# Hybrid trunk layer on one core: tile 8's left half last, a ring of three left blocks, evenly paced weight sums

## The chip, the cores and the metric

The kernel runs on one core of one Trainium2 chip. Times are device microseconds of one launch, the median of several runs. TensorE (PE) multiplies matrices, VectorE (DVE) and ScalarE (ACT) work on SBUF and PSUM, GpSimd (POOL) on SBUF; DMAs are issued from the queues of SyncE (SP), ACT and POOL. The engines run beside one another and wait by semaphores; each works through its own instructions in order.

## What is computed

One layer of a diffusion trunk on 9 tiles of 128 tokens: tiles 0 to 7 are the 1024 latent tokens, tile 8 holds 128 context tokens. The layer normalises and modulates its input, projects it, forms a gated chunk MLP (group A) and a 4-head latent attention (group B), and ends with one output projection. Only the attention and this end matter here:

```python
p = jax.nn.softmax(s, axis=-1)                       # s: 1024 latent + 256 cached keys
attn = jnp.einsum('bhqk,bkhv->bqhv', p, v_all)
y = jnp.concatenate([a_out, attn * silu(g_b)], axis=-1) @ w_o     # 1024 x 1024
out = x + gate * y                                    # gate by condition: latent or context
y_final = rmsnorm(out, final_g)                       # over the 1024 columns
```

## The kernel before

Every product in float32 is made of three matmuls: each operand is split into a high part (a cast, fp32r) and a low part (the rest), and high x high, high x low and low x high are summed in PSUM. `lo_of` (L112, DVE) makes a low part; the high part is a cast on ACT or `pool_copy` (L115) on POOL.

**Output projection.** The mixed activations lie in `mixA` (group A) and `mixB` (group B), transposed. Tiles 0 to 7 form four pairs. A pair's 2 x 2 block product with `w_o` (token tile x half of the inputs, against half of the inputs x half of the columns) is done by Strassen and Winograd's scheme with 7 products in place of 8. A product has 4 steps of 128 inputs, each 3 matmuls of 128x512 (`three`, L1909 to L1911), 12 in all. Its left block is a block of activations (`A11`, `A12`, `A22`) or a sum of blocks (`S1` to `S4`, made on POOL by `s_sums`); its right block is a quarter of `w_o` (`B11`, `B21`, `B22`) or one of four combinations `T1` to `T4`. Results are added up as `c11`, `c12`, `c21`, `c22`, then gated (`m..`), added to `x` (`a..`), squared with a row sum (`sq`), normalised (`norm`) and scaled by `final_g` (`y`, L2110). Tile 8 has no partner: `out_terms` (L1938 to L1940) does it with 8 steps of 3 matmuls for each half of 512 columns, early, as filler between the last attention heads.

**Left blocks.** `ring(q)` gives product q one of five SBUF slots for its high and low part; the cast into it, a copy `raw` into PSUM (L2136) and the subtraction (L112) come ahead of the product.

**Weight combinations.** `t_unit` makes T1 to T4 during attention in 8 units (u) of two half steps. A unit has four subtractions on POOL (L809), two casts on ACT into `thi` (L1883), two low parts on DVE in place in `traw`, and eight stores to `tdram` on SP (L1880). `divide` runs once per head and calls one or two half steps in turn. After the units, the rows of `w_o` are loaded (`wo_piece`, L1653) through one raw buffer at a time and split, two pieces per head (`spare_hi`, `spare_lo`). The combinations come back by DMAs on POOL's queue: `t_fetch` (L1901) for T3 and `t_piece` (L1905) for the others.

**Order.** In attention, one list of steps for PE sets the order, with due times (`later`) for what other engines do. After attention a small planner (`Plan.run`) goes through the steps with their costs, dependencies and priorities and writes each engine's instructions in that order; nothing is reordered when it runs. Pieces of tile 8 and of the first two products (`early`, one piece is 3 matmuls) stand among the last heads' matmuls.

**The end.** The last product, `A22` of pair 3, is done in two pieces of 256 columns, and tile 7's sum of squares is completed with the second.

Of the kernel before, what the change touches and what calls it, by code (L numbers as in the profile page):

```python
# [94 lines left out]
def tile_hymba_step(ctx: ExitStack, tc: tile.TileContext, I, O):  # L95
# [1371 lines left out]
    units, traw, unit_of, paced = [], {}, [], [0]  # L1467
    s2 = pss.tile([P, 2, 256], F32, tag="s2", name="s2", bufs=1)

    def softmax(t, h, lat_, con_):  # L1470
# [22 lines left out]
        def divide():  # L1493
            V.tensor_tensor(rs, su[:, 0:1], su[:, 1:2], op=ALU.add)
            V.reciprocal(rs, rs)  # L1495
            G.tensor_scalar(e, e, rs, 0.0, op0=ALU.mult, op1=ALU.add)  # L1496
# [140 lines left out]
    raw_free = [True]  # L1637
# [6 lines left out]
    def next_load():  # L1644
        if not loads or (loads[0][0] < 5 and not raw_free[0]):
            return
        k, hi, lo = loads.pop(0)
        if k < 5:
            raw_free[0] = False
            r = wo.tile([P, 1024], F32, tag="wor", name=f"wor{k}", bufs=1)  # L1650
        else:
            r = ap_.tile([P, 1280], F32, tag="e", name=f"wor{k}", bufs=6)[:, :1024]
        nc.sync.dma_start(r, I["w_o"][k])  # L1653

        def low(c_):
            lo_of(lo[:, c_], r[:, c_], hi[:, c_])
            if c_.start and k < 5:
                raw_free[0] = True
                next_load()
# [123 lines left out]
    with tc.manual_schedule(engines=engines):  # L1783
# [11 lines left out]
        EARLY = (("A11", "B11"), ("A12", "B21"), ("S4", "B22"), ("S2", "T2"), ("S1", "T1"), ("S3", "T3"), ("A22", "T4"))  # L1795
        FINAL = (("A11", "B11"), ("A12", "B21"), ("S2", "T2"), ("S1", "T1"), ("S3", "T3"), ("S4", "B22"), ("A22", "T4"))
        queue = [(n, *blk) for n in range(4) for blk in (FINAL if n == 3 else EARLY)]
# [19 lines left out]
        def ring(q):  # L1817

            i = q % 5
            if i not in slots:  # L1820
# [3 lines left out]
                    3: lambda: flat[0][4], 4: lambda: wo.tile([P, 1024], F32R, tag="ml", name="ringA", bufs=2),  # L1824
# [22 lines left out]
        def need_lo(key):  # L1847
            while key not in made:
                if los:
                    spare_lo(1)  # L1850
                else:
# [3 lines left out]
                    now[0] = now_  # L1855

        th, tl = {}, {}
# [7 lines left out]
        def t_unit(u, part):  # L1865
# [3 lines left out]
            b11, b12, b21, b22 = (raw[:, i, :] for i in range(4))  # L1869
            if part == 0:  # L1870
# [5 lines left out]
            hi = tp.tile([P, 4, 256], F32R, tag="hi", name=f"thi{u}")  # L1876

            def store(i, src):
                for m, j in ((1, 0), (3, 1), (4, 2), (2, 3)):
                    nc.sync.dma_start(f32(tdram[m - 1, k][:, i, 256 * c : 256 * c + 256]), src[:, j, :])  # L1880

            def high(i):
                S.copy(hi[:, 2 * i : 2 * i + 2, :], raw[:, 2 * i : 2 * i + 2, :])  # L1883
                if i:
                    store(0, f32(hi))

            def low(i):
                lo_of(raw[:, 2 * i : 2 * i + 2, :].bitcast(F32R), raw[:, 2 * i : 2 * i + 2, :], hi[:, 2 * i : 2 * i + 2, :])
                if i:
                    store(1, raw)  # L1890
                    if u + 2 < 8:
                        t_load(u + 2)

            for i in range(2):
                later(3.2 + 1.8 * i, lambda i=i: high(i))
                later(4.6 + 1.8 * i, lambda i=i: low(i))
# [48 lines left out]
        for c in range(len(pairs)):  # L1945
# [18 lines left out]
            if 2 * c + LEAD + 1 == 17:  # L1964
                assert not units
                closed(c_tp)
                c_wo, wo = opened("wo", side="left")
                for k in range(2):
                    wo_piece(k, *flat[0][2 * k : 2 * k + 2])
# [12 lines left out]
        wps[8] = [psw.tile([P, 512], F32, tag="w", name=f"w8{i}") for i in range(2)]  # L1982
        first_banks = [psw.tile([P, 512], F32, tag="w", name=f"f{i}") for i in range(2)]

        def load_xr(t):
            xr[t] = ep.tile([P, 1024], F32, tag="xr", name=f"xr{t}", bufs=4)
            nc.sync.dma_start(xr[t], I["x"][t])

        def plain(k, i):
            out_terms(8, wps[8][i], 512 * i, 512 * i + 512, [k])  # L1990
            if k == 4 and i == 1:
                for n in range(4):
                    t_fetch(3, n, woh[n][:, 512:1024], wol[n][:, 512:1024])

        early = []
        for k in range(7):
            early += [(0.65, lambda i=i, k=k: plain(k, i)) for i in range(2)]
            if k < 4:
                early.append((0.65, lambda k=k: product(0, first_banks[0], ks=[k])))
            elif k < 6:  # L2000
                early.append((0.65, lambda k=k: product(1, first_banks[1], ks=[k - 4])))
# [33 lines left out]
    def on_g(key, fn, deps, prio, cost=1.3, **kw):  # L2035
        step(key, "G", cost, fn, deps, prio, lag=0.15, **kw)
# [8 lines left out]
    def load_gate(cond, **kw):  # L2045
        gate[cond] = ep.tile([P, 1024], F32, name=f"gate{cond}", **kw)
        nc.sync.dma_start(
            gate[cond].rearrange("p (j r) -> p j r", j=4), gdram.rearrange("j (c r) -> c j r", c=2)[cond : cond + 1].broadcast_to([P, 4, 256])
        )

    for m, n in ((1, 0), (4, 4)):
        for k in range(4):
            fetch(f"T{m}{k}", lambda m=m, k=k, n=n: t_piece(m, k, tpiece[n + k]))
        if m == 1:
            fetch("gate0", lambda: load_gate(0, tag="gate0"))
    fetch("gate1", lambda: load_gate(1, tag="xr", bufs=4))
    for t in (8, 0, 1):
        fetch(f"x{t}", lambda t=t: load_xr(t))
    fetch("fg", lambda: nc.sync.dma_start(fg, I["final_g"].broadcast_to([P, 1024])))
# [9 lines left out]
    groups = {t: g for g in ((8,), (0, 1), (2, 3), (4, 5), (6,), (7,)) for t in g}  # L2069

    def square(t, j, junk, c, deps, prio=3.0, src=None):
        g = groups[t]

        def go():
            if g not in ssq:
                ssq[g] = sm.tile([P, 4], F32, tag="fss", name=f"fss{t}", bufs=3)
# [12 lines left out]
    def norm(g, prio, by_half=False):  # L2089
# [16 lines left out]

        for i, u in enumerate(g):
# [5 lines left out]
            if not by_half:  # L2113
                on_v(f"y{u}", scale, [*prev, "fg"], prio, 1.25)

        def scale_half(c):
            S.activation(xr[t][:, c], xr[t][:, c], AF.Copy, scale=ssq[g][:, 0:1])  # L2117
            nc.scalar.dma_start(O["y"][t][:, c], xr[t][:, c])

        if by_half:  # L2120
            for h_, c in (("L", L), ("R", R)):
                on_s(f"y{t}{h_}", lambda c=c: scale_half(c), [*prev, f"fg{t}{h_}"], 1.5)
# [4 lines left out]
    for q in range(3, len(queue)):  # L2127
# [4 lines left out]
        room = {3: ["pl7"], 4: ["pl7"], 5: []}.get(q) if q < 6 else [name_of(q - 5)]  # L2132
# [20 lines left out]
    def finish_plain():  # L2153
        for j, c in enumerate((L, R)):
            ps = wps[8][j]
            on_v(f"g8{j}", lambda ps=ps, c=c: V.tensor_tensor(ps, ps, gate[1][:, c], op=ALU.mult), ["pl7", "gate1"], 3.0)
            on_v(f"a8{j}", lambda ps=ps, c=c: V.tensor_tensor(xr[8][:, c], ps, xr[8][:, c], op=ALU.add), [f"g8{j}", "x8"], 3.0)
            square(8, j, lambda ps=ps: ps, c, [f"a8{j}"])
        step("free8", "N", 0.0, lambda: None, ["sq8.0", "sq8.1"], 0, gives=("w", "w"))
        norm((8,), 3.5)  # L2160
# [3 lines left out]
    def pair(n):  # L2164
# [3 lines left out]
        last = n == 3  # L2168
# [3 lines left out]
        q0 = 7 * n  # L2172
        at_ = {queue[q0 + i][1]: q0 + i for i in range(7)}
# [7 lines left out]
        for i in range(6 if last else 7):  # L2181
            q = q0 + i
            name = queue[q][1]
            m = queue[q][2]
            deps = [f"lo{q}", *([f"{m}{k}" for k in range(4)] if m[0] == "T" else [])]
            if n == 0 and i < 2:
                banks[name] = first_banks[i]
                if i == 0:
                    plan.made[P_(name)] = plan.made["|" + P_(name)] = 0.0
                    continue  # L2190

                def rest(q=q, name=name):
                    product(q, banks[name], ks=[2])
                    for h_ in range(2):
                        plain(7, h_)
                    plan.made["pl7"] = 2.4
                    product(q, banks[name], ks=[3])

                on_t(P_(name), 2.75, rest, [])
                continue  # L2200

            def whole(q=q, name=name):
                bank(name)
                product(q, banks[name])

            on_t(P_(name), 2.73, whole, deps, takes=("w",))

# [3 lines left out]
        if last:  # L2211
            on_v(D_("m11"), lambda: V.tensor_tensor(banks["A12"], banks["A12"], gate[0][:, L], op=ALU.mult), [D_("c11")], 2)
            on_v(D_("a11"), lambda: V.tensor_tensor(xr[a][:, L], banks["A12"], xr[a][:, L], op=ALU.add), [D_("m11"), f"x{a}"], 2)
            square(a, 0, lambda: banks["A12"], L, [D_("a11")])
            step(f"free{n}", "N", 0.0, lambda: None, [f"sq{a}.0"], 0, gives=("w",))
        else:
# [195 lines left out]
```

## Time and profile before

| | |
|---|---|
| median of 3 runs | 629.32 us (628.65 to 631.04) |
| the profiled execution | 629.55 us, its span 627.8 us |
| PE busy | 600.1 us (96%) |
| DVE, ACT, POOL busy | 68%, 53%, 35% |
| mean granted PE clock | 0.992 |
| attention, heads | until about 536 us |
| output products | PE's last matmul ends at 615.78 us |

Times in the profile count from the span's start. "Busy" is the time in which an engine executes; the idle time before an instruction is given with what released it, in square brackets in the timeline. An engine that is idle costs time only if PE, or the last chain, waits for it.

### The profile page before, as it was taken

To read this page: it belongs to the slowest core of one execution; us is meant where nothing else is said; L and a number is where in the kernel's file an instruction comes from. 1 tells how busy PE (TensorE), PEld (TensorE's weight loads), DVE (VectorE), ACT (ScalarE), POOL (GpSimd) and SP (SyncE) were. 2 spreads that over 40 slices of the span, in tenths; PEclk is the share of its full clock that TensorE was granted. 3 is DMA by queue.
4 is the path that set the end of the run, shared out by engine and by line. 5 is a ranking of instruction groups with operands and counts; after the bars stand their busy time and mean duration, and the time that the engine had idled before them with its cause. 6 is when DMAs were issued, how large, how long until landed. Compare 5 with 4: busy or idle time off the path is not lost. (4 is left out here: it accounts for less than half of the span.)

```text
span 627.8 us, 10196 instructions
## 1 busy us (share of the span) xinstructions
PE 600.1 (96%) x3659; PEld 538.9 (86%) x3659; DVE 427.5 (68%) x911; ACT 329.9 (53%) x765; POOL 218.1 (35%) x261
## 2 busy tenths in 40 slices
PE   8899999999999999999999989899999999989992
PEld 7578889999989999999988978789999988768882
DVE  4784458896855567566778677786766855458765
ACT  6556754336423354555675656566555443456543
POOL 2451111000000000433462455552332566558772
PEclk9999999999999999999999999999999999989997
DMA  8992000101261034000020063651101028944222
GB/s 318 389 367 72 1 33 2 34 1 67 101 232 62 11 119 131 13 1 1 6 69 1 27 215 130 202 167 35 68 2 34 33 85 267 367 154 168 88 101 114
DMA packets 31922, 67.33 MB, mean 107 GB/s; under 512 B 3440, under 2 KB 18560, under 8 KB 31360
## 3 DMA queue, kind: packets, MB, share of 16 engines
q1 hardware_dynamic: 28560, 57.50, 26.5%
q0 software_dynamic: 2880, 8.39, 4.1%
q10 hardware_dynamic: 432, 0.79, 0.3%
q8 instruction: 29, 0.48, 0.3%
q14 instruction: 21, 0.17, 0.1%
HBM read 53.45 MB, written 13.21 MB: 106 GB/s over the span
## 5 line engine op out<-in xcount | busy, mean ns | idle before, releaser
L1496 POOL TENSOR_SCALAR e<-e,rs 128x1280 f32<-128x1280 f32 x32 | 46.2, 1444 | 105.5 <-DVE rs L1495 49.3
L112 DVE TENSOR_TENSOR pl<-pT,ph 128x512 fp32r<-128x512 f32 x81 | 55.4, 687 | 39.3 <-ACT ph L1561 37.9
L1490 ACT ACTIVATE e<-s,nb,scl 128x256 f32<-128x256 f32 x64 | 56.1, 880 | 39.8 <-DVE nb L1484 39.8
L1561 ACT CAST ph<-pT 128x512 fp32r<-128x512 f32 x80 | 46.0, 587 | 35.4 <-PE pT L1557 31.7
L1237 POOL TENSOR_TENSOR kr<-z,rope 128x64 f32<-128x64 f32 x8 | 2.6, 322 | 172.5 <-ACT z L1246 172.5
L1557 PE MATMUL pT<-ident,e 128*128 128x128 f32 x320 | 48.4, 274 | 6.8 <-DVE pl L112 6.8
L752 PE MATMUL tp<-area,w 128*128 128x384 f32 x288 | 52.4, 338 | 0.0
L752 PEld LDWEIGHTS tp<-area,w 128*128 128x128 f32 x288 | 50.3, 188 | 0.4
L1581 PE MATMUL o<-ph,vh 128*128 128x256 f32 x160 | 47.7, 298 | 0.0
L1557 PEld LDWEIGHTS pT<-ident,e 128*128 128x128 f32 x320 | 37.1, 140 | 12.1 <-PE at L1600 4.0
L1583 PE MATMUL o<-ph,vl 128*128 128x256 f32 x160 | 45.2, 282 | 0.0
L1582 PE MATMUL o<-pl,vh 128*128 128x256 f32 x160 | 45.1, 282 | 0.0
L1480 DVE TENSOR_REDUCE m<-s 128x1 f32<-128x1024 f32 x32 | 38.9, 1216 | 1.5 <-PE s L1514 1.5
L1510 PE MATMUL s<-kch,area 128*128 128x512 f32 (+2 forms) x100 | 39.0, 390 | 0.0
L1513 PE MATMUL s<-krh,area 128*128 128x512 f32 (+2 forms) x100 | 35.4, 354 | 0.0
L1511 PE MATMUL s<-kcl,area 128*128 128x512 f32 (+2 forms) x100 | 35.3, 353 | 0.0
L1512 PE MATMUL s<-kch,area 128*128 128x512 f32 (+2 forms) x100 | 35.2, 352 | 0.0
L1514 PE MATMUL s<-krl,area 128*128 128x512 f32 (+2 forms) x100 | 35.2, 352 | 0.0
L976 PE MATMUL tp<-area,w 128*128 128x384 f32 x192 | 35.0, 337 | 0.0
L976 PEld LDWEIGHTS tp<-area,w 128*128 128x128 f32 x192 | 33.6, 188 | 0.4 <-issue 0.4
L1581 PEld LDWEIGHTS o<-ph,vh 128*128 128x128 f32 x160 | 30.4, 190 | 1.6
L1582 PEld LDWEIGHTS o<-pl,vh 128*128 128x128 f32 x160 | 30.4, 190 | 1.4
(660 smaller groups left out, 1731.3 us busy)
## 6 DMA issues: line engine op xcount, KB each, us to landing
ada<-in_ada_ss SPq DMA_DIRECT2D x16, 512.0 KB, 8.5
w2r<-in_w_t SPq DMA_DIRECT2D x12, 512.0 KB, 4.5
x<-in_x SPq DMA_DIRECT2D x9, 512.0 KB, 7.9
xr<-in_x SPq DMA_DIRECT2D x9, 512.0 KB, 8.5
adag<-in_ada_g SPq DMA_DIRECT2D x4, 1024.0 KB, 5.0
traw<-in_w_o SPq DMA_DIRECT2D x16, 256.0 KB, 3.4
tdram<-thi SPq DMA_DIRECT2D x32, 128.0 KB, 3.0
tdram<-traw SPq DMA_DIRECT2D x32, 128.0 KB, 2.1
```

Of the source, the lines that this page charges most:

```text
L112: V.tensor_tensor(lo, src, f32(hi), op=ALU.subtract)
L752: T.matmul(tps[i, g][:, :GW], w_[i][:, k, :], x_[k, g], start=k == 0 and j == 0, stop=k == NK - 1 and j == 2)
L976: T.matmul(tps[c, 2][:, :GW], w_[c][:, k, :], x_[k, 2], start=k == 0 and m == 0, stop=k == NK - 1 and m == 2)
L1480: V.tensor_reduce(m[:, 0:1], lat_, axis=AX.X, op=ALU.max)
L1490: S.activation(e[:, sl], src, AF.Exp, bias=nb, scale=scl[:, t : t + 1], accum_out=su[:, i : i + 1])
L1496: G.tensor_scalar(e, e, rs, 0.0, op0=ALU.mult, op1=ALU.add)
L1510: T.matmul(ps, qh_, kch[:, sl], start=True, stop=False)
L1557: T.transpose(ps[:, w : w + P], es[t, h][:, c * P : (c + 1) * P], ident)
L1561: later(0.5, lambda: S.copy(ph[:, :w], ps[:, :w]))
L1581: T.matmul(o, vh[:, kt, :], ph[:, sl], start=c == 0, stop=False)
L1582: T.matmul(o, vh[:, kt, :], pl[:, sl], start=False, stop=False)
L1583: T.matmul(o, vl[:, kt, :], ph[:, sl], start=False, stop=c == n - 1)
```

## The change

It does these things:

- `t_unit`: `divide` calls one half step per head, always. `thi` becomes two tiles of half the size; each half is stored by two DMAs as soon as it is made. The raw rows of `w_o` open after the last unit, wherever that falls, and are read through two buffers instead of one (`raw_free` holds two tags).
- Tile 8's right half stays among the early pieces; its left half is moved behind the last product, in two pieces of 256 columns. Three steps of the third product join the early pieces. The early list has 17 pieces instead of 20.
- `ring` has three slots instead of five (the slot of tile 8's own high part stays taken until the end). A product's left block waits for the product three before it.
- The order of the products is written out for the first nine (`FIRST`): pair 1's first two products come ahead of pair 0's `A22`.
- C21 stays in its PSUM bank and is gated and added to `x` there by DVE, for all pairs, instead of POOL in SBUF.
- `gate0`, tile 8's gate and input (`own1`), `x0`, `x1` and `final_g` are loaded from ACT's queue instead of SP's, later in the order; tile 8's gate and input are loaded by halves.
- Tiles 6 and 7 are normalised together, and the last sums are those of tile 8.

What it does to the order at three places. SP's stores and loads in the weight sums, before (`tdram<-thi` are the high parts, `tdram<-traw` the low parts, `traw<-in_w_o` the next unit's rows):

```order
L1880 DMA tdram<-thi_4268 128x256 x4
L1880 DMA tdram<-traw_4113 128x256 x4
L1863 DMA traw_4368<-in_w_o 128x2x256 x2
L1880 DMA tdram<-thi_4354 128x256 x4
L1880 DMA tdram<-traw_4275 128x256 x4
L1863 DMA traw_4452<-in_w_o 128x2x256 x2
```

and after:

```order
L1876 DMA tdram<-thi_4354 128x256 x2
L1876 DMA tdram<-traw_4095 128x256 x2
L1876 DMA tdram<-thi_4385 128x256 x2
L1876 DMA tdram<-traw_4095 128x256 x2
L1867 DMA traw_4416<-in_w_o 128x2x256 x2
```

A unit's stores are the same eight, in pairs, and two tiles of high parts take turns.

POOL at the end of attention, before (`area` and `kch`, `krh` are places of `w_o` rows, `tp`, `vht`, `vlt` those of T1 and T4):

```order
L1905 DMA area_120<-tdram 128x1024 x4
L115 TENSOR_SCALAR kch_5755<-wor_5757 128x512 x2
L115 TENSOR_SCALAR krh_5759<-wor_5761 128x512 x2
L115 TENSOR_SCALAR area_120<-wor_5763 128x512
L1901 DMA area_118<-tdram 128x512 x4
L1901 DMA area_119<-tdram 128x512 x4
L115 TENSOR_SCALAR area_120<-wor_5763 128x512
L115 TENSOR_SCALAR ringC<-mixB 128x512
L1905 DMA tp_6044<-tdram 128x1024
L1905 DMA tp_6045<-tdram 128x1024
L1905 DMA tp_6046<-tdram 128x1024
L1905 DMA tp_6047<-tdram 128x1024
```

```order
L806 TENSOR_TENSOR mixA<-mixA,mixB 128x4x128
L1905 DMA tp_6048<-tdram 128x1024
L809 TENSOR_TENSOR mixB<-mixA 128x4x128
L1905 DMA tp_6049<-tdram 128x1024
L809 TENSOR_TENSOR mixA<-mixA 128x4x128
L1905 DMA vht<-tdram 128x1024
L809 TENSOR_TENSOR mixB<-mixB 128x4x128
L1905 DMA vlt<-tdram 128x1024
```

and after, from the same place:

```order
L115 TENSOR_SCALAR area_120<-wor_5771 128x512 x2
L1911 DMA area_118<-tdram 128x512 x4
L1911 DMA area_119<-tdram 128x512 x4
L115 TENSOR_SCALAR ringC<-mixB 128x512
L1915 DMA tp_6043<-tdram 128x1024
L1915 DMA tp_6044<-tdram 128x1024
L1915 DMA tp_6045<-tdram 128x1024
L1915 DMA tp_6046<-tdram 128x1024
L1915 DMA tp_6047<-tdram 128x1024
L1915 DMA tp_6048<-tdram 128x1024
L1915 DMA vht<-tdram 128x1024
L1915 DMA vlt<-tdram 128x1024
```

The fetches of T1 and T4 stand in one run, and pair 1's sums come behind them.

DVE at the end, before (L2283, L2284 gate and add the last product's two pieces; L2254, L2255 are tile 6's, L2300 is tile 7's output):

```order
L2110 SCALAR_TENSOR_TENSOR xr_6349<-xr_6349,fss_6485,fg 128x1024
L2110 SCALAR_TENSOR_TENSOR xr_6371<-xr_6371,fss_6485,fg 128x1024
L2263 TENSOR_TENSOR P_3_6665<-S_3_6630,gate_6100 128x512
L2267 TENSOR_TENSOR S_3_6630<-S_3_6630,gate_6100 128x512
L2268 TENSOR_TENSOR xr_6532<-S_3_6630,xr_6532 128x512
L2266 TENSOR_TENSOR xr_6532<-P_3_6665,xr_6532 128x512
L806 TENSOR_TENSOR S_3_6652<-S_3_6652,mixB 128x512
L2283 TENSOR_TENSOR A_3_6670<-A_3_6670,gate_6100 128x256
L2254 TENSOR_TENSOR S_3_6652<-S_3_6652,gate_6100 128x512
L2284 TENSOR_TENSOR A_3_6670<-A_3_6670,xr_6532 128x256
L2283 TENSOR_TENSOR A_3_6670<-A_3_6670,gate_6100 128x256
L2255 TENSOR_TENSOR xr_6510<-S_3_6652,xr_6510 128x512
```

and after (`left` is tile 8's left half, `own_6610` its gate and input, `A_3` the last product):

```order
L806 TENSOR_TENSOR A_3_6633<-A_3_6633,mixA 128x512
L2221 TENSOR_TENSOR A_3_6633<-A_3_6633,gate_6094 128x512
L2222 TENSOR_TENSOR xr_6514<-A_3_6633,xr_6514 128x512
L2273 TENSOR_TENSOR left<-left,own_6610 128x256
L2098 TENSOR_TENSOR smalls<-smalls,fss_6586 128x2
L2274 TENSOR_TENSOR left<-left,own_6610 128x256
```

```order
L2120 SCALAR_TENSOR_TENSOR xr_6491<-xr_6491,fss_6586,fg 128x1024
L2273 TENSOR_TENSOR left<-left,own_6610 128x256
L2277 TENSOR_SCALAR smalls<-smalls 128x1
L2274 TENSOR_TENSOR left<-left,own_6610 128x256
L2281 SCALAR_TENSOR_TENSOR smalls<-fss_6187,smalls 128x1
L2283 RECIPROCAL rlast<-smalls 128x1
```

Tile 6's output scaling (L2120) now stands ahead of the last piece's gating; tile 7's work is ahead of it.

The diff, cut to its core:

```diff
-                n_ = min(len(units), (1, 2)[paced[0] % 2])
+                n_ = 1
                 paced[0] += 1
-                for _ in range(n_):
-                    unit_of[0](*units.pop(0))
+                for i in range(n_):
+                    unit_of[0](*units.pop(0), 2.2 * i)
...
-    raw_free = [True]
+    raw_free = ["wor", "ml"]
...
+        FIRST = ((0, "A11"), (0, "A12"), (0, "S4"), (0, "S2"), (0, "S3"), (0, "S1"), (1, "A11"), (1, "A12"), (0, "A22"))
+        LATER = {1: ("S1", "S2", "S4", "S3", "A22"), 2: ("A11", "A12", "S2", "S1", "S4", "S3", "A22"), 3: ("A11", "A12", "S2", "S1", "S3", "S4", "A22")}
...
-            i = q % 5
+            i = q % 3
             if i not in slots:
                 slots[i] = {
                     0: lambda: flat[0][5], 1: lambda: wo.tile([P, 1024], F32R, tag="ml", name="ringB", bufs=2),
                     2: lambda: wo.tile([P, 1024], F32R, tag="wor", name="ringC", bufs=1),
-                    3: lambda: flat[0][4], 4: lambda: wo.tile([P, 1024], F32R, tag="ml", name="ringA", bufs=2),
...
+            def store(i, part_, src):
+                for m, j in ((1, 0), (3, 1), (4, 2), (2, 3))[2 * i : 2 * i + 2]:
+                    nc.sync.dma_start(f32(tdram[m - 1, k][:, part_, 256 * c : 256 * c + 256]), src[:, j % 2, :])
+
+            def high(i):
+                his_[u, i] = tp.tile([P, 2, 256], F32R, tag=f"hi{i}", name=f"thi{u}{i}")
+                S.copy(his_[u, i], raw[:, 2 * i : 2 * i + 2, :])
+                store(i, 0, f32(his_[u, i]))
...
+            for dt, fn, i in ((3.2, high, 0), (4.6, low, 0), (5.0, high, 1), (6.4, low, 1)):
+                later(dt + more, lambda fn=fn, i=i: fn(i))
...
+        early = [(0.65, lambda k=k: plain(k)) for k in range(4)]
+        early += [(0.65, lambda k=k: product(0, first_banks[0], ks=[k])) for k in range(4)]
+        for k in range(3):
+            early.append((0.65, lambda k=k: plain(4 + k)))
+            early.append((0.65, lambda k=k: product(1, first_banks[1], ks=[k])))
+        early += [(0.65, lambda k=k: product(2, first_banks[2], ks=[k])) for k in range(3)]
...
+    def load_gate():
+        gate[0] = ep.tile([P, 1024], F32, name="gate0", tag="gate0")
+        nc.scalar.dma_start(
...
-            on_v(D_("c21"), lambda: add(V, K, ps("A22"), K), [P_("A22"), D_("k7")], 2, gives=("w",))
-            on_g(D_("m21"), lambda: G.tensor_tensor(K, K, gL(), op=ALU.mult), [D_("c21"), "gate0"], 3)
-            on_g(D_("a21"), lambda: add(G, half(b, L), half(b, L), K), [D_("m21"), f"x{b}"], 3)
...
+            on_v(D_("c21"), lambda: add(V, ps("A22"), ps("A22"), K), [P_("A22"), D_("k7")], 2)
+            on_v(D_("m21"), lambda: V.tensor_tensor(banks["A22"], banks["A22"], gate[0][:, L], op=ALU.mult), [D_("c21"), "gate0"], 2.5)
+            on_v(D_("a21"), lambda: V.tensor_tensor(xr[b][:, L], banks["A22"], xr[b][:, L], op=ALU.add), [D_("m21"), f"x{b}"], 2.5)
...
+        def left(j, c):
...
+            out_terms(8, cell["o"][:, c], c.start, c.stop, range(8))
+
+        for j, c in enumerate((slice(0, 256), slice(256, 512))):
+            on_t(f"pz{j}", 2.9, lambda j=j, c=c: left(j, c), [], takes=("w", "w") if j == 0 else ())
+            on_v(f"zm{j}", lambda c=c: V.tensor_tensor(cell["o"][:, c], cell["o"][:, c], g()[:, c], op=ALU.mult), [f"pz{j}", "own0"], 0.5, 0.42)
+            on_v(f"za{j}", lambda c=c: V.tensor_tensor(cell["o"][:, c], cell["o"][:, c], x()[:, c], op=ALU.add), [f"zm{j}"], 0.5, 0.42)
```

More of the change, by code (lines that the diff above doesn't have):

```diff
@@ L1644, in next_load @@
     def next_load():
-        if not loads or (loads[0][0] < 5 and not raw_free[0]):
+        if not loads or (loads[0][0] < 5 and not raw_free):
             return
@@ L1657, in low @@
             if c_.start and k < 5:
[L1658 removed]
+                raw_free.append(tag)
                 next_load()
@@ L1875, in t_unit, with open_wo @@
             sub(G, b21, b21, b22)
[L1876 to L1896, printed above, removed]
+            for dt, fn, i in ((3.2, high, 0), (4.6, low, 0), (5.0, high, 1), (6.4, low, 1)):
+                later(dt + more, lambda fn=fn, i=i: fn(i))
+        def open_wo():
+            nonlocal c_wo, wo
+            closed(c_tp)
+            c_wo, wo = opened("wo", side="left")
+            for k in range(2):
+                wo_piece(k, *flat[0][2 * k : 2 * k + 2])
         def t_fetch(m, k, hi, lo):
@@ L2179, in bank @@
             banks[name] = psw.tile([P, 512], F32, tag="w", name=f"{name}_{n}")
[L2181 to L2206, printed above, removed]
+        bank_of[n] = bank, banks
         s_done = [f"s{m}{n}" for m in range(4)]
```

278 lines of the change are left out of this document (141 added, 137 removed).

## The prediction

> **What bounds the kernel now.** I read the page first, then the waits of PE, then busy time by stretch, then the timeline at each gap and the chain that ended last. The page says that PE is the engine that matters, and that no other is near full:
>
> ```profile
> PE 600.1 (96%) x3659; PEld 538.9 (86%) x3659; DVE 427.5 (68%) x911; ACT 329.9 (53%) x765; POOL 218.1 (35%) x261
> ```
>
> So time is won or lost only where PE stands still, and after its last matmul. The stretches show where (columns: PE, PEld, DVE, ACT, POOL busy, PE clock, DMA share, GB/s):
>
> ```profile
> 350.00:360.00 10.00, 10.00 (x70) 9.12 (x70) 6.16 (x14) 6.61 (x14) 4.21 (x5) 1.00 0.08 28
> 360.00:380.00 20.00, 17.39 (x118) 15.55 (x117) 15.36 (x30) 12.03 (x26) 10.66 (x11) 1.00 0.62 198
> 380.00:400.00 20.00, 19.50 (x136) 17.74 (x135) 14.71 (x26) 11.94 (x26) 11.96 (x13) 1.00 0.48 159
> 400.00:430.00 30.00, 27.50 (x189) 24.93 (x189) 22.77 (x45) 17.97 (x38) 13.41 (x13) 1.00 0.51 158
> 430.00:500.00 70.00, 70.00 (x491) 64.63 (x489) 50.27 (x105) 39.24 (x83) 23.58 (x24) 1.00 0.09 31
> 540.00:560.00 20.00, 17.33 (x68) 13.21 (x67) 12.52 (x20) 9.14 (x20) 13.35 (x13) 0.91 0.77 272
> 560.00:616.00 56.00, 55.78 (x258) 46.49 (x256) 41.41 (x75) 30.32 (x72) 39.57 (x28) 1.00 0.35 122
> 616.00:627.80 11.80, 0.00 (x0) 0.00 (x0) 5.39 (x20) 4.41 (x13) 2.53 (x2) 0.71 0.24 89
> ```
>
> Three losses lie in what the change touches. PE idles 2.61 + 0.50 + 2.50 = 5.6 us between 360 and 430, where the weight sums run, and nothing in the 70 us after. It loses 2.7 us at 540 to 560. It ends at 615.78 (0.22 short of 616), and 12.0 us follow without it. The profiled execution took 629.55 us, 0.23 above the median of the runs, with 1.75 us around its span of 627.8; the sum below is made against 629.55.
>
> **1. Weight sums in attention: one half step per head, stores by halves.** What PE and ACT wait for there:
>
> ```profile
> PE pT L1557 <- DVE pl L112: 6.8, 10, 1.1
> ACT thi L1883 <- DMA tdram<-thi: 4.6, 3, 2.8
> ACT thi L1883 <- DMA tdram<-traw: 2.8, 1, 2.8
> L1883 ACT CAST thi<-traw x16: 609/622/635, 354.7 to 419.2; 128x512 fp32r<-128x512 f32 x16
> L1496 POOL TENSOR_SCALAR e<-e,rs x28: 1334/1349/1630, 339.7 to 511.7; 128x1280 f32<-128x1280 f32 x28
> ```
>
> PE's transposes wait for `pl`, which waits for the cast `ph` on ACT; ACT works in order, and there the cast `thi` stands before it, up to 2.8 us, until the last unit's stores have left the one `thi` buffer (or `traw` has left its own). The division of `e` comes once per head, so a head lasts (511.7 - 339.7) / 27 = 6.4 us. With 1, 2, 1, 2 half steps per head a unit follows the last one after 6.4 or 12.7 us; now it is always 12.7, each half of `thi` has its own tile, and its stores leave at once. A wait of at most 2.8 us ends inside the 6.3 us added, so I take 4.8 us of the 5.6 as gained; the rest I leave, since one PE gap of this kind lies before the first unit. Ends: 0 (units that close up for another reason) and 5.6. The units now run until about 354 + 16 x 6.4 = 456, and the rows of `w_o`, read after them, fall into consecutive heads; the row 430 to 500 holds such rows too and PE is full there, so this costs nothing while DVE stays near 50.27 of 70.
>
> **2. Products on T1 and T4.** The two gaps of PE after attention, with the matmuls that follow the second:
>
> ```profile
> 546.05 0.47 PE L1909 MATMUL S<-tp,ringA 128*128 128x512 f32 x1 [0.83 <-ACT area L2138]
> 555.94 0.65 PE L1909 MATMUL A<-vlt,ringB 128*128 128x512 f32 x1 [1.84 <-DMA vlt<-tdram]
> 556.39 0.63 PE L1910 MATMUL A<-vlt,ringB 128*128 128x512 f32 x1
> ...
> 559.70 0.40 PE L1909 MATMUL A<-area,ringC 128*128 128x512 f32 x1
> 547.60 0.57 POOL L1905 DMA_DIRECT2D vlt<-tdram  x1
> vlt<-tdram POOLq DMA_DIRECT2D x1, 512.0 KB, 8.3
> ```
>
> T4's last piece is issued at 547.60, since POOL's left-block sums stand between the fetches, and lands 8.3 us later, too late for product 7. Now all eight fetches of T1 and T4 stand in one run (8 x 0.57 = 4.6 us from about 533) and T4 is needed only by the ninth product, at about 553: landing by 538 + 8.3 = 546, the 1.84 us go. After that gap nine matmuls take 559.70 - 555.94 = 3.76 us instead of 9 x 0.23 = 2.07, 1.7 us of slow clock, which I count as the gap's and as gone with it. Together 3.5 (ends 0 and 3.5). The 0.83 before the S1 product goes too: S1 is now the sixth product, behind a T3 product that needs only rows fetched before. Ends 0 and 0.83; taken 0.8.
>
> The slow stretch follows 1.84 us of idle time. The Trainium skill ("TensorE: Matmul & The Clock Gate", What's actually happening) lets the array fall to half clock only after an idle window of about 3.4 us; by that rule the slow stretch is not the gap's, would stay, and the sum would be 1.7 us higher. The trace has the clock at 1.00 in every other stretch shown while PE works, so I follow the trace.
>
> **3. Tile 8's left half last.** It takes 24 matmuls of 512 columns out of the early stage (24 x 0.23 = 5.5 us) and puts 48 of 256 at the end; the kernel's last matmuls of that width give the price:
>
> ```profile
> 615.26 0.28 PE L1909 MATMUL A<-vlt,ringC 128*128 128x256 f32 x1
> 615.38 0.28 PE L1910 MATMUL A<-vlt,ringC 128*128 128x256 f32 x1
> ```
>
> 48 x 0.12 = 5.7 us, so nothing changes in sum. What it costs is cover at the start. The third product (left block in `ringC`) now begins before the last head is done:
>
> ```profile
> 525.49 0.62 POOL L115 TENSOR_SCALAR area<-wor 128x512 fp32r<-128x512 f32 x1 [4.88 <-DMA wor<-in_w_o]
> 526.05 4.29 POOL L1901 DMA_DIRECT2D area<-tdram  x8
> 530.30 0.70 POOL L115 TENSOR_SCALAR area<-wor 128x512 fp32r<-128x512 f32 x1
> 530.89 0.69 POOL L115 TENSOR_SCALAR ringC<-mixB 128x512 fp32r<-128x512 f32 x1
> 531.08 1.05 DVE L112 TENSOR_TENSOR area<-wor,area 128x512 fp32r<-128x512 f32 x1
> 531.75 0.60 PE L1557 MATMUL pT<-ident,e 128*128 128x128 f32 x4
> ```
>
> On POOL the eight fetches of T3 (4.29 us) still stand ahead of the cast into `ringC`: 525.49 + 2 x 0.6 + 4.29 + 0.7 = 531.7, then 0.69 on DVE: 532.4. PE has 17 early pieces before that head's last transposes, then and now (20 in all before), so it arrives at 531.75 less 0.7, at 531.05, and waits 1.35 us, with those transposes behind. The left block of the fourth product is copied on ACT after the last `os` copy and split on DVE behind the last multiplication of attention: 0.42 + 0.69 on DVE against 0.69 + 0.46 of matmuls, about 0.5 us more. Cost 1.9; ends 0 (a `w_o` row that lands sooner) and 4.
>
> The loads: `gate0`, tile 8's right part, `x0`, `x1` and `fg` are now issued by ACT, between casts (seven issues of 0.35 us, beside a PE that is fed two products ahead, so nothing by themselves). DVE's first gating waits for `gate0`, and behind it stand the split for the eighth product and the release of a bank that PE needs for the seventh.
>
> ```profile
> gate<-gdram SPq DMA_DIRECT2D x2, 512.0 KB, 9.8
> xr<-in_x SPq DMA_DIRECT2D x6, 512.0 KB, 3.4
> 540.71 0.62 ACT L2138 CAST ringB<-mixB 128x512 fp32r<-128x512 f32 x1
> ```
>
> With the start stage 3.6 us shorter (5.5 less 1.9) the seventh product begins near 547.3. `gate0` is issued near 540.8, after the fourth to sixth casts, and takes between 3.4 (empty queues) and 9.8 us (in company of 7 MB): it is there at 544.2 to 550.6. The fetches are over by about 546, so I take 545.5 and no wait; the late end would cost 550.6 + 0.7 - 547.3 = 4.0.
>
> **4. Ring of three.** A left block can be made only once the product three before has ended. Its chain is short:
>
> ```profile
> 542.36 0.62 ACT L2138 CAST ringC<-mixA 128x512 fp32r<-128x512 f32 x1 [0.55 <-PE S L1910]
> 542.88 0.58 ACT L2136 COPY raw<-mixA 128x512 f32<-128x512 f32 x1
> 543.50 0.69 DVE L112 TENSOR_TENSOR ringC<-raw,ringC 128x512 fp32r<-128x512 f32 x1 [0.97 <-ACT raw L2136]
> 608.43 4.28 DVE L2110 SCALAR_TENSOR_TENSOR xr<-xr,fss,fg 128x1024 f32<-128x1024 f32 x2
> ```
>
> 1.9 us against two products of 12 x 0.23 = 2.73 each, 5.5 us: 3.6 us to spare. Two scalings of output tiles back to back on DVE (4.28) are the one thing that outlasts it, by 0.7, once per pair for three pairs: 0 to 2.1 us; the scalings now mostly stand apart, with a split between them, so I take 1.0. C21's gating in PSUM adds 2 x 0.69 us of DVE for three pairs (4.1) and removes one half of tile 8's (1.4): some 44 of 56 us, cover enough; POOL loses 1.29 x 2 per pair.
>
> **5. The tail.** Before, one chain of DVE and ACT runs from 612.63 to the end, behind those 4.28 us, and tiles 6 and 7 finish together:
>
> ```profile
> 621.74 0.76 DVE xr L2300
> 622.59 0.73 ACT xr L2304
> 623.73 0.72 ACT xr L2117
> 624.48 0.34 ACTq L2118 DMA_DIRECT2D out_y<-xr  x1
> ```
>
> Now the 5.7 us of tile 8 lie between the last product and PE's end E. The last product ends at E - 5.7; three gatings of 0.69, a square of some 0.8 and a norm of some 1.8 behind it end at E - 1.0; y6 (one scaling, 1.3 to 2.1) stands ahead of the last gating on DVE, and two halves of y7 with their issues (2 x 1.1) ahead of the last square on ACT, so that square ends at E + 1.9 to 2.5. The rest is as before: root, reciprocal and refinement 1.25, output half 0.75, issue 0.34, and 627.8 - 624.82 = 3.0 to land. E + 7.3 to 7.9 against 12.0; gain 4.3 (ends 2, both halves of y7 late, and 4.7).
>
> **Sum:** -4.8 - 3.5 - 0.8 + 1.9 + 1.0 - 4.3 = -10.5: 629.55 - 10.5 = 619.05, and against the median 618.8.
>
> **Rivals.** (a) *Late loads*: `gate0` or tile 8's part comes at the 9.8 us end and PE waits at the seventh to twelfth product, 4.0 us and perhaps a slow stretch: 623 to 625. For it: two loads in the trace took so long; against: less else is in flight. (b) *The weight sums still stall PE*, because DVE and POOL there (15.36 and 10.66 of 20) and not the stores set the pace: +4.8, 623.6. Against: ACT's rows name the stores for 7.4 of its wait. (c) *No gain in the tail*, tile 7's and tile 8's norms in each other's way on ACT: +4.0, 622.8. (d) *The slow clock stays*: its cause lies elsewhere than in the gap, and it strikes wherever it will: +1.7, 620.5. The page of the Trainium skill named in part 2 ("TensorE: Matmul & The Clock Gate") speaks for it. (e) *Slower*: the ring of three makes PE wait at nearly every product, because casts and splits queue behind squares, scalings and gatings. It decides when a left block comes over 0.45 us late at each of the 23 products from the sixth on (10.5 / 23), that is when its chain takes 3.6 + 0.45 = 4.1 us longer than 1.9; at 0.9 us each it is 618.8 + 20.7 = 639.5. DVE, busy 41.41 of 56 before, speaks for some queueing; ACT's 30.32 against.
>
> **How the numbers follow.** Forecast 0.56 (its own range 615 to 623), (a) 0.10, (b) 0.10, (c) 0.05, (d) 0.05, (e) 0.14. The best ends give 629.3 - 13.5 = 615.8; the range goes from 615 to 628, where two of (a) to (c) meet, and leaves out (e) and little else. About 0.5%, 3.1 us, is what a measurement of this kernel can tell from no change. Faster: the forecast and 0.20 of the 0.30 in (a) to (d), 0.76; the 0.10 in which two of them meet is the same; slower 0.14.
>
> **What would show it.** Right: PE waiting for `pl` under 2 us in all; no wait for `vlt` and no clock under 1.00 after attention; PE idle near 531 behind `ringC`; about 7.7 us from PE's last matmul to the span's end. Wrong: PE waits on `ringA/B/C` splits or a bank freed by DVE spread over the products; `gate0` landing after 547; ACT still waiting for `tdram` in 360 to 460.

## The result and the profile after

| | before | after |
|---|---|---|
| median of 20 runs each | 628.91 us | 625.97 us |
| lowest to highest | 625.48 to 633.13 | 624.39 to 628.06 |
| the profiled execution | 629.55 (span 627.8) | 624.43 (span 622.7) |

The ratio is 0.9955, with a 95% interval of 0.9937 to 0.9973: 2.8 us faster (1.7 to 4.0). The forecast was 10.5 us. Of the 20 runs after, the 12 with a mean granted clock of 0.989 or more took 624.4 to 626.4 us, the 8 below it 626.5 to 628.1; the profiled one is of the first kind.

The two profiles stand 5.1 us apart, more than the medians. The code ahead of attention is the same in both, yet the first long exponential of attention ends its wait at 319.55 in the one and 318.00 in the other; over all profiles of this study that point lies between 318.0 and 321.1. So stages are compared from fixed points of the program, read from the timelines: the first head's long exponential (e), tile 8's first matmul (w), the last `os` copy (o), PE's end (start of its last matmul and 0.28), the end of the span.

| us | e to w | w to o | o to PE's end | PE's end to the end |
|---|---|---|---|---|
| before | 190.4 | 26.0 | 79.9 | 12.0 |
| after | 185.4 | 25.9 | 82.4 | 11.0 |

So attention gave 5.0 us and the tail 1.0, and the stage of the products took 2.5 back. What PE waited for after the change, from 340 on:

```profile
PE A L1919 <- DVE mixB L2195: 4.0, 1, 4.0
PE pT L1558 <- DVE pl L112: 3.1, 9, 0.9
PE f L1921 <- DVE ringC L112: 0.3, 1, 0.3
```

The waits for T4 and for the S1 product are gone, the waits for `pl` have halved, and one new wait of 4.0 us has come. It stands ahead of the seventh product, for the bank that DVE's first gating (L2195) frees. Timeline rows of ACT, DVE, PE and POOL around it (start, duration, in brackets the idle time before and what ended it):

```profile
531.56 0.40 ACTq L2050 DMA_DIRECT2D gate<-gdram  x1
542.77 0.69 DVE L2195 TENSOR_TENSOR mixB<-f,gate 128x512 f32<-128x512 f32 x1 [7.00 <-DMA gate<-gdram]
543.61 0.47 PE L1919 MATMUL A<-area 128*128 128x512 f32 x1 [3.96 <-DVE mixB L2195]
526.65 3.25 POOL L1915 DMA_DIRECT2D tp<-tdram  x6 [3.40 <-PE pT L1558]
530.35 0.60 POOL L1915 DMA_DIRECT2D vlt<-tdram  x1
```

`gate0` leaves ACT's queue at 531.56 and is there at 542.77, 11.2 us later. PE's stretches of 2 us behind it (PE, PEld, DVE, ACT, POOL busy, granted PE clock, DMA share, GB/s):

```profile
540.00:542.00 2.00, 0.00 (x0) 0.00 (x0) 0.00 (x0) 0.72 (x2) 0.00 (x0) 1.00 1.10 382
542.00:544.00 2.00, 0.39 (x2) 0.38 (x3) 1.23 (x3) 0.00 (x0) 0.00 (x0) 1.00 1.00 294
544.00:546.00 2.00, 2.00 (x8) 1.58 (x7) 1.97 (x5) 0.00 (x0) 0.53 (x1) 0.68 1.02 400
546.00:548.00 2.00, 2.00 (x6) 1.54 (x6) 1.97 (x4) 0.18 (x1) 2.00 (x3) 0.50 0.30 117
548.00:550.00 2.00, 2.00 (x10) 1.67 (x9) 1.21 (x2) 1.58 (x4) 2.00 (x2) 0.97 0.51 180
```

Lost clock: 0.32, 0.50 and 0.03 of 2 us each, 1.7 us. The DMA engines are full (1.10, 1.00, 1.02) until after the gate has landed. The tail, from the timelines of PE, DVE and ACT:

```profile
611.39 0.28 PE L1950 MATMUL left<-area,ml 128*128 128x256 f32 x1
611.71 0.43 DVE L2273 TENSOR_TENSOR left<-left,own 128x256 f32<-128x256 f32 x1 [3.59 <-PE left L1950]
613.87 1.27 DVE L2120 SCALAR_TENSOR_TENSOR xr<-xr,fss,fg 128x1024 f32<-128x1024 f32 x1
615.07 0.42 DVE L2273 TENSOR_TENSOR left<-left,own 128x256 f32<-128x256 f32 x1
618.58 0.37 ACTq L2294 DMA_DIRECT2D out_y<-wuv  x1
```

The first piece of tile 8's left half ends 2.9 us before PE's end, and DVE's gating of it begins only at PE's end, with the norm of tiles 6 and 7 behind it on DVE.

### The profile page after: what moved, and what is told of

It reads as the page before. It is cut to its first block, busy times and chain, and to the rows that moved or that the text cites. A ratio compares the mean times of both kernels' runs of the same rounds, so it can differ in the third digit from the quotient of the medians.

```text
span 622.7 us, 10205 instructions
## 1 busy us (share of the span) xinstructions
PE 599.6 (96%) x3671; PEld 540.6 (87%) x3671; DVE 427.5 (69%) x909; ACT 329.6 (53%) x763; POOL 209.2 (34%) x254
## 3 DMA queue, kind: packets, MB, share of 16 engines
q10 hardware_dynamic: 1808, 3.41, 1.6%
## 4 chain that ended last, share of the span: by engine, by line
PE 80%; DVE 10%; ACT 4%; DMA 3%; issue 2%; SPq 0%; ACTq 0%
PE p L954 10%; PE tp L752 8%; PE tp L976 5%; PE pT L1558 4%; DVE pl L112 3%; PE zacc L1390 2%; PE zacc L1389 2%; PE zacc L1391 2%; PE s L1512 2%; PE s L1514 2%; PE s L1513 2%; PE s L1511 2%; PE s L1515 2%; DMA gate<-gdram 2%; PE o L1584 2%
```

## The experiments

Each kernel ran beside the kernel before on the same chip, and each ratio is to that. Not all experiments ran on one chip, so they are compared by their ratios.

**Gate from SP's queue.** After, with

```diff
-        nc.scalar.dma_start(
+        nc.sync.dma_start(
             gate[0].rearrange("p (j r) -> p j r", j=4), gdram...
```

> Edit: gate0 is issued from SP's queue instead of ACT's; nothing else moves. Theory (late gate): in the changed kernel gate0 leaves ACT's queue at 531.56 and lands 11.2 us later, PE stands 4.0 us before the seventh product, and the 4.3 us of matmuls behind that gap run at half speed, 2.0 us more. From SP it can leave at about 528, as soon as its place in SBUF is free, and lands by 538 to 540: PE waits 0 to 0.5 us there, no slow stretch follows, the time falls by 5 to 6 us against the changed kernel. Rival (shared transfers): the landing is set by the 4.2 MB of T1 and T4 in front of it, whatever queue issues it; it lands at 542 to 543 again, or T1 lands later by the same and the sixth product waits, and the time falls by under 1.5 us.

Measured: 624.91 us, ratio 0.9924 (0.9895 to 0.9952). This profile started 3.1 us later than that of the changed kernel (e at 321.13); there:

```profile
532.50 0.38 SPq L2050 DMA_DIRECT2D gate<-gdram  x1
544.38 0.69 DVE L2195 TENSOR_TENSOR mixB<-f,gate 128x512 f32<-128x512 f32 x1 [5.42 <-DMA gate<-gdram]
```

Issued right after the last `os` copy instead of 2.2 us behind it, it took 11.9 us; the gap is 2.4 us, and a slow stretch still follows (0.91 in 540 to 560). The theory missed: the queue decided little. By the ratios the time fell by 1.9 us against the changed kernel, a little more than the rival's 1.5. That the eight fetches in front set the landing, as the rival has it, is tested below (gate in front of the fetches).

**Two banks for tile 8's left half.** After, with

```diff
-                cell["o"] = psw.tile([P, 512], F32, tag="w", name="left")
-                cell["junk"] = psw.tile([P, 512], F32, tag="w", name="junk")
-            out_terms(8, cell["o"][:, c], c.start, c.stop, range(8))
+                cell[0] = psw.tile([P, 512], F32, tag="w", name="left0")
+                cell[1] = psw.tile([P, 512], F32, tag="w", name="left1")
+            out_terms(8, cell[j][:, c], c.start, c.stop, range(8))
...
```

> Edit: the two pieces of tile 8's left half go to two PSUM banks instead of one (the squares' waste goes to the unused halves, the last scaling on DVE becomes two of 256 columns). Theory (bank wait): DVE's gating of the first piece waits for PE's last matmul into the same bank, 2.9 us later than its own, and the norm of tiles 6 and 7 stands behind it in DVE's order, which is why 11.0 us follow PE's end instead of the 7.7 of the forecast. With two banks the first gating starts 2.9 us before PE's end, and 8.0 to 8.8 us follow it: 2.2 to 3.0 us off the changed kernel's time. Rival (queue): what follows PE's end is the work of ACT and DVE itself (y6, two halves of y7, the square, the refinement), and the wait only hides it: under 1 us off.

Measured: 624.3 us, 0.9911 (0.9884 to 0.9938). DVE's rows:

```profile
612.07 0.43 DVE L2273 TENSOR_TENSOR left<-left,own 128x256 f32<-128x256 f32 x1 [0.72 <-PE left L1950]
614.21 1.27 DVE L2120 SCALAR_TENSOR_TENSOR xr<-xr,fss,fg 128x1024 f32<-128x1024 f32 x1
615.40 0.42 DVE L2273 TENSOR_TENSOR left<-left,own 128x256 f32<-128x256 f32 x1
```

The first gating begins at 612.07, 2.8 us ahead of PE's end at 614.90, and 8.0 us follow that end instead of 11.0. The bank theory holds, at the upper end. By the ratios the time fell by 2.8 us, by the medians by 1.7. The profile also has a slow stretch twice as long as the changed kernel's behind the gap before the seventh product (last section), which takes part of the gain back.

**Both together.**

> Both edits together: gate0 from SP's queue and two banks for tile 8's left half. If both theories hold the gains add, since one lies before the seventh product and the other behind the last: 7 to 9 us off the changed kernel's time, about 617 to 619 us where the changed kernel takes 626. If the rivals hold, under 2.5 us off.

Measured: 619.78 us, 0.9849 (0.9819 to 0.9878). The tail is 7.9 us. The gap is still 2.7 us, with no slow clock behind it in the profile; that, not the end of the gap, is why the time came close to what was expected, so the agreement is in part luck.

**The weight sums alone, in the kernel before.** The new `t_unit`, one half step per head, `w_o`'s rows opened after the last unit.

> Edit: the kernel before with the weight sums of the changed kernel alone (one half step per head, two half-size tiles for the high parts, stores by halves, w_o's rows opened after the last unit, still through one raw buffer). Theory: PE's idle time at the transposes falls from 5.6 us in 360 to 430 to about 1.2, and with the output stage unchanged the time falls by 4 to 5 us against the kernel before. Rival (given back): the gain is taken back where the output stage waits for T4's fetch or for the rows of w_o, and the time falls by under 2 us.

Measured: 624.75 us, 0.9921 (0.9891 to 0.995), with e to w 185.4 us. The theory holds in attention. T4's fetch then held PE for 3.0 us instead of 1.8, so a little was given back.

**The old pace in the changed kernel.** After, with

```diff
-                n_ = 1
+                n_ = min(len(units), (1, 2)[paced[0] % 2])
```

> Edit: the changed kernel with the old pace, one and two half steps per head in turn; the two half-size tiles and the early stores stay. Theory (pace): units that follow after one head still close up, and of the 4.4 us of PE idle time gained in 360 to 430 most comes back: PE waits for pl 5 us or more in all, the time rises by 3 to 4.5 us against the changed kernel. Rival (tiles): it was the single tile of high parts alone that held ACT, the pace gave nothing, and the wait stays under 3.5 us, the time within 1 us of the changed kernel's.

Measured: 634.07 us, 1.007 (1.0043 to 1.0098), e to w 192.0 us: 6.6 more than after, and not less than before. ACT never waits for a store here, and PE stands still all the same: from 340 on it waits 7.2 us for `pl`, against 3.1 after. Behind its longest gap in attention the granted clock is 0.50 for 3.4 us (380.34 to 383.75), another 1.7 us. That gap, and DVE and POOL in front of it:

```profile
374.27 1.42 DVE L112 TENSOR_TENSOR traw<-traw,thi 128x512 fp32r<-128x512 f32 x1
375.62 1.21 DVE L1481 TENSOR_REDUCE m<-s 128x1 f32<-128x1024 f32 x1
376.75 0.89 DVE L112 TENSOR_TENSOR traw<-traw,thi 128x512 fp32r<-128x512 f32 x1
378.14 0.68 DVE L112 TENSOR_TENSOR pl<-pT,ph 128x512 fp32r<-128x512 f32 x1
375.12 1.97 POOL L809 TENSOR_TENSOR traw<-traw 128x256 f32<-128x256 f32 x2
378.98 0.63 PE L1558 MATMUL pT<-ident,e 128*128 128x128 f32 x4 [1.92 <-DVE pl L112]
```

DVE has no free moment from 372.66 on: two low parts of the unit stand ahead of `pl`. They take 1.42 and 0.89 us, where 13 of the 16 low parts take 0.67 to 0.84; POOL's division of `e` and two of its subtractions run beside them; that this is why they are long was not tested. This is not the kernel before with other tiles, though. Where a head has two half steps, the second one's casts and low parts are due 2.2 us later than there. The two longest gaps (1.92 and 1.74 us) stand at the two units that this moves; their two casts lie 1.0 us apart (372.52 and 373.52, 401.08 and 402.08), those of the kernel before 2.7. So the run shows that the half-size tiles don't mend the old pace; it doesn't show how the old pace cost time before.

**Three slots in the kernel before.** `i = q % 3` and the rooms that go with it.

> Edit: the kernel before with three left-block slots instead of five, all else as before. Theory (the ring is free): a left block takes 1.9 us and has two products, 5.5 us, for it; PE shows no wait on a ring slot or split behind 560, and the time is within 1 us of the kernel before. Forecast's term: about 1.0 us of waits where scalings on DVE outlast the slack. Rival (e) of the forecast: waits at many products, 4 us or more in all.

Measured: 627.96 us, 0.9979 (0.9961 to 0.9996). Behind attention PE has no wait on a slot or split; its only gap there is the 0.8 us of the S1 product. With this order T4's last piece lands in time, the stage from o to PE's end takes 75.9 us, and the tail 14.0, 2.0 more than before; DVE's order at the end has changed too, and this was not taken apart. For PE the ring is free.

**Gate in front of the fetches.** Two banks, SP's queue, and `gate0`'s tile laid out ahead of T1's and T4's:

```diff
+    gate[0] = ep.tile([P, 1024], F32, name="gate0", tag="gate0")
     tpiece = [ep.tile([P, 1024], F32R, tag=f"t{i}", name=f"tp{i}") for i in range(6)]
...
```

> Edit: two banks for tile 8's left half as before, and gate0 from SP's queue into a tile laid out ahead of T1's and T4's, so that its place is free one step earlier: it can be issued at about 526.6, together with T1's first fetch and not behind all eight. Theory (the fetches in front set the landing): gate0 lands 5 to 8 us after its issue, by 535, before the seventh product needs it at 539.6; PE has no gap there, no slow clock follows in 540 to 560, and the time is 2.7 us or more under that of the kernel with gate0 from SP's queue behind them (619.8), about 616 to 617. Rival (slow by itself): a broadcast of 512 KB from so few bytes takes 11 to 12 us wherever it stands; it lands at 538, the gap goes all the same, but only just. Second rival: T1 now lands later by gate0's share and the sixth product waits 1 us or more.

Measured: 618.21 us, 0.9816 (0.9789 to 0.9843); only the run with seven gatings, below, is level with it. DVE's wait, from the timelines:

```profile
528.34 0.38 SPq L2050 DMA_DIRECT2D gate<-gdram  x1
537.61 0.68 DVE L2195 TENSOR_TENSOR mixB<-f,gate 128x512 f32<-128x512 f32 x1
```

and the stretch behind it (columns as above):

```profile
540.00:550.00 10.00, 10.00 (x45) 8.17 (x44) 5.73 (x9) 3.76 (x8) 3.37 (x3) 1.00 1.02 356
```

The gating no longer waits, so `gate0` took 9.3 us or less; the gap and the slow clock are gone, and T1 came no later for PE. From o to PE's end it takes 77.3 us against 82.4 after. Two things took the wait away: `gate0` left 2.9 us ahead of the last `os` copy and not right behind it, and its flight was at least 2.6 us shorter than the 11.9 from the same queue behind the fetches. The second rules out that it is slow by itself. Against both edits together the time fell by 2.1 us by the ratios, a little less than the 2.7 expected.

**The new pace alone, with the old tiles.** The kernel before with `n_ = 1`, and `w_o`'s rows opened after the last unit.

> Edit: the kernel before with the new pace alone, one half step per head; the high parts stay in one tile of full size, stored at the end of the unit. Theory (pace): what held PE was DVE, where the low parts of a unit and the subtractions of POOL crowded into one head; with one half step per head attention shrinks by about 5 us (first exponential to tile 8's first matmul 185.4 us instead of 190.4) with the old tiles too, and PE waits for pl about 3 us in all. Forecast's reading (stores): the single tile still makes ACT's cast wait for the stores, up to 2.8 us; part of the idle time stays, 1.5 us or more of the 5.

Measured: 624.2 us, 0.9932 (0.9905 to 0.996), e to w 185.2 us, and no wait of ACT for a store. The pace gives the whole gain in attention; the half-size tiles give nothing more. Between stores and DVE the run does not decide: at the new pace the waits for stores are gone with the old tiles too, as the forecast's sum had it (6.3 us more between units, and waits of at most 2.8).

**A gap made by DVE.** The kernel with the gate in front, its first gating done seven times over (the same values again):

```diff
-            on_v(D_("m11"), lambda: V.tensor_tensor(C, ps("A12"), gL(), op=ALU.mult), ...
+            on_v(D_("m11"), lambda: [V.tensor_tensor(C, ps("A12"), gL(), op=ALU.mult) for _ in range(1 if n else 7)], ...
```

> Edit: the fastest kernel so far (gate0 in front, two banks; 618.2 us), with the first gating on DVE done seven times over instead of once (the same result each time), so that the bank for the seventh product comes free about 2 us late. No transfer is involved. It asks whether the slow matmuls come of the gap or of the transfers that were in flight at the gaps seen so far. Theory (gap): PE stands some 2 us near 540, and behind it the matmuls run at half speed for 3.4 us or twice that in most runs: 3.5 to 5.5 us over 618.2. Rival (transfers): the clock stays 1.00, the time is 618.2 plus the gap, about 620.

Measured: 617.77 us, 0.9833 (0.9787 to 0.988); the gap was only 1.2 us and the clock stayed 1.00. It tells nothing between the two. With eleven:

> Edit: as the run with seven gatings, with eleven, so that the gap before the seventh product is about 4 us (1.22 and four times 0.72), as long as the one in the changed kernel, and again caused by DVE alone. Theory (gap): a slow stretch of 3.4 or 6.8 us follows, as in the changed kernel; the mean clock falls to 0.985 to 0.991 and the time is 617.8 + 2.9 for the gap + 1.7 or 3.4, 622.4 to 624.1. Rival (transfers): the clock stays 0.993 or more, the time is 620 to 621.

Measured: 622.89 us, 0.9893 (0.9863 to 0.9922). Stretches of 2 us:

```profile
542.00:544.00 2.00, 0.00 (x0) 0.00 (x0) 1.90 (x4) 0.46 (x1) 0.00 (x0) 0.82 0.95 267
544.00:546.00 2.00, 0.85 (x2) 0.78 (x3) 1.97 (x4) 0.00 (x0) 0.00 (x0) 0.50 0.85 256
546.00:548.00 2.00, 2.00 (x6) 1.52 (x6) 1.97 (x4) 0.00 (x0) 0.99 (x1) 0.50 0.89 361
548.00:550.00 2.00, 2.00 (x7) 1.52 (x6) 1.97 (x4) 0.00 (x0) 2.00 (x3) 0.50 0.18 64
550.00:552.00 2.00, 2.00 (x10) 1.67 (x9) 0.61 (x2) 1.71 (x4) 2.00 (x3) 0.97 0.41 100
```

A gap of 4.1 us that no transfer caused brings the slow clock, with the DMA engines no fuller (0.85 to 0.95) than with the gate in front (1.02), where the clock stayed 1.00: the gap theory holds. The mean clock was 0.992 in two of its four runs, a little above the 0.991 expected at most, and 0.989 and 0.991 in the others.

## Why the prediction was wrong

The direction was right and the size was not: 2.8 us where 10.5 were forecast, under half. Point by point, with stages from the profiles:

- **Weight sums.** Size right: 5.0 against 4.8, and the pace alone gives it. How the old pace costs the time is open. The forecast put it on the stores that hold ACT's cast. The rows of the kernel before bear that out at its two longest gaps there, 1.14 and 1.11 us; at the first,

```profile
370.50 0.62 ACT L1883 CAST thi<-traw 128x512 fp32r<-128x512 f32 x1 [2.82 <-DMA tdram<-traw]
372.76 0.58 ACT L1561 CAST ph<-pT 128x512 fp32r<-128x512 f32 x1
373.37 0.69 DVE L112 TENSOR_TENSOR pl<-pT,ph 128x512 fp32r<-128x512 f32 x1 [1.47 <-ACT ph L1561]
374.12 0.66 PE L1557 MATMUL pT<-ident,e 128*128 128x128 f32 x4 [1.14 <-DVE pl L112]
```

  Here DVE stands idle for `ph`, which ACT makes late. At the three gaps of 0.73 or 0.74 us DVE is busy right up to `pl`. With the old pace and half-size tiles the waits for stores are gone and PE waits for DVE, but that run also moves units; with the new pace both kinds go. So neither the forecast's stores nor rival (b)'s DVE and POOL is shown as the whole cause, and (b)'s consequence, no gain, did not come.
- **T4 and S1.** Right: both waits are gone. But the slow clock did not go with T4's gap: it came back behind the new one.
- **Start stage.** Forecast 1.9 us; PE's waits there are 0.3, and w to o is unchanged (25.9 against 26.0). The last row of `w_o` was split 9.1 us ahead of the last head's transposes (516.73 to 525.87) where the sum had 6.3, so `ringC` was filled in time.
- **Loads: the step that failed most.** The sum took `gate0` to land 4.7 us after its issue, when the eight fetches would be nearly over, and no wait. It landed after 11.2, with 4.0 us of gap and 1.7 of slow clock: rival (a), at its upper end, given 0.10. The forecast's own late end, 9.8 us, was 1.4 short, but the 4.0 us of waiting that it priced were right; the choice went by "less is in flight". In fact all eight fetches were issued in one run ahead of it, which the change itself did: the pieces of T4 took 12.0 and 13.0 us to land (`vht`, `vlt`) where they had taken 8.1 and 8.3. The forecast's sign for this, a landing after 547, could not have told: all of this stage came earlier (the last `os` copy at 529.32 and not at 535.90), so a landing at 542.77 was already late.
- **Ring of three.** Forecast 1.0; PE's waits on a left block behind 530 are none.
- **Tail: the second step that failed.** Forecast 7.7 us, measured 11.0. The sum let DVE gate the first piece when PE had done it; the gating waits for PE's last matmul into the bank. The kernel before could not show this: its last product has two pieces too, but DVE was busy without a break from 612.63 until it gated the first of them (L2283) at 615.82. With two banks the tail is 7.9 to 8.0.

Together: gap and slow clock +5.7, tail +3.3, start -1.6, ring -1.0, weight sums -0.2 make +6.2 on a sum of -10.5, -4.3; the profiles, less the 1.55 us that lie ahead of attention, show -3.6, and 0.7 us is not placed. With both faults mended the kernel takes 618.21, against the 618.8 forecast. That is close in part by luck, since the start stage and the ring cost 2.6 us less than the forecast had for them. One sum of the forecast is wrong without bearing on this: its best ends add up to 14.6 us, not 13.5.

## What to carry to other kernels

When a change bundles transfers into one run, ask what small load is issued behind them and who waits for it: here 4.2 MB of fetches that were early enough cost 4 us through a 0.5 MB load that was not. When work is cut into two pieces so that the second hides the first's epilogue, look whether the two write one PSUM bank, since the reader may wait for both. And a wait with a name in the profile is a suspect, not a cause: removing it alone is the test, and only if the run leaves everything else where it was.

## What the runs showed of the hardware

The slow clock behind a gap of PE looks unsteady by the gap's length. Gaps of 0.8 (three slots), 1.2 (seven gatings), 0.8 and 1.4 (pace alone) and 1.74 us (old pace) had none behind them; 1.84 (before), 1.92 (old pace), 2.4 (SP's queue) and 3.0 us (weight sums alone) had one; 2.1 (three slots) and 2.7 us (both edits) had none. At 3.9 to 4.1 us there was one each time, once short and three times long.

The traces' records of the granted clock settle it. In each profile every change of the clock behind the first 20 us lies a whole number of lengths of 3.41 us from the others: in the changed kernel 21 lengths from the slow stretch at 544.72 to the one in the tail at 616.40. Whether the next length is slow follows from how long PE works in the present one. Columns as above; first the changed kernel, then both edits, then two banks:

```profile
541.30:544.72 3.42, 1.11 (x5) 0.96 (x6) 1.91 (x4) 0.00 (x0) 0.00 (x0) 1.00 1.03 331
544.72:548.13 3.41, 3.41 (x10) 2.66 (x9) 3.38 (x6) 0.32 (x1) 2.66 (x3) 0.50 0.56 219
539.02:542.43 3.41, 1.85 (x8) 1.14 (x7) 0.00 (x0) 1.23 (x3) 0.00 (x0) 1.00 1.12 401
542.43:545.84 3.41, 2.24 (x10) 1.86 (x11) 3.04 (x5) 0.00 (x0) 0.39 (x1) 1.00 0.96 335
541.38:544.80 3.42, 0.32 (x2) 0.00 (x0) 0.00 (x0) 1.21 (x2) 0.00 (x0) 1.00 1.16 376
544.80:548.21 3.41, 2.57 (x6) 2.12 (x7) 3.38 (x6) 0.00 (x0) 0.72 (x1) 0.50 0.93 347
548.21:551.62 3.41, 3.41 (x9) 2.64 (x9) 2.29 (x4) 0.84 (x2) 3.41 (x4) 0.50 0.19 55
```

With 1.11 us of work the next length is slow. With both edits the grid cuts the gap of 2.7 us in two, 1.85 and 2.24 us of work remain, and nothing follows. Over the 12 profiles, behind 20 us, all 20 lengths at full clock with 1.57 us of work or less (12 of them in the tail) have a slow one behind them, and none of the 2060 with 1.59 us or more. The two nearest the limit, from the kernel before and from three slots:

```profile
552.73:556.14 3.41, 1.57 (x6) 0.69 (x5) 2.17 (x4) 0.00 (x0) 3.41 (x3) 1.00 0.42 148
401.15:404.56 3.41, 1.59 (x14) 1.59 (x15) 2.31 (x6) 2.90 (x7) 1.18 (x1) 1.00 0.62 179
```

A slow length with 3.25 us of work or more has full clock behind it; with 2.57 or less a second slow one follows, as with two banks, where the gap reached into the slow length. So, as an estimate from 1.58 of 3.41 us: alone, a gap under 1.8 us brings no slow clock, one over 3.7 us always does, and between the two it hangs on where the grid cuts it.

Lengths of 3.4 us fit what the Trainium skill says ("TensorE: Matmul & The Clock Gate", What's actually happening): the clock follows a free-running window of about 3.4 us. Its condition, a window of idle, was not needed here: in the kernel before, 1.84 us of idle time within one length were enough. The forecast's rival (d), that the slow clock has another cause than the gap, is answered: without the gap it was gone, and a gap made by DVE alone brought it back.
